# One decoder layer with product-key experts: table rows on one DMA queue, and the samples' retention in two halves of a buffer

## The chip, the cores and the metric

The kernel runs on one core of one Trainium2 chip, as one launch. The metric is the device time of an execution in microseconds, lower is better. A core has TensorE (PE; its weight loads are shown as PEld), VectorE (DVE), ScalarE (ACT), GpSimd (POOL) and SyncE (SP). A DMA is asked for by an instruction in one engine's queue; in the profile `ACTq` and `SPq` are such instructions, and the transfers of each asking engine form a queue of their own (q1 for SyncE, q10 for ScalarE, q0 for GpSimd's gathers).

## What is computed

One layer of a hybrid decoder for 512 tokens of a prompt and for 32 tokens of samples (8 samples of 4 tokens), width 1024. The input projection gives queries, keys, values and gates of a retention of four heads (head size 128), and the input of a causal depthwise convolution of width 31. Both halves are joined by an output projection, a residual and a normalisation. Then each token takes 16 of 16,384 experts for each of 8 heads, found by product keys. Cut to the parts that the change is near:

```python
# retention, for each chunk (a sample is one chunk of 4 tokens)
r_new   = chunk_decay * r + kv                  # state 128 x 128 for each sample and head
o_cross = einsum('bnihd,bnhde,hi->bnihe', qc, r_prev, decay_in)
# experts
u   = take(peer_u, idx)                         # (tokens, heads, 16, 1024)
act = gelu(einsum('phkd,pd->phk', u, x))
vv  = take(peer_v, idx)
out = einsum('phk,phkd->pd', gate * act, vv)
```

The outputs are the layer's result for prompt and samples, the new retention states and the new convolution caches.

## The kernel before

**The front, up to about 480 us.** The projection runs in blocks of tokens, the samples beside one of the prompt's. `retain_s` (L384 to L424) is the retention of the samples. After a first product over all 32 tokens (L396) it walks over four pairs of samples. For each pair it takes one buffer of the pool tag `keys` (L400, `keys_or_scratch`, one buffer); ScalarE writes the pair's values, scaled so that only the sample's own tokens are left, into the second half of it (L403); ScalarE's queue loads the pair's states, 1 MB, into the first half (L404). Eight matmuls take the states into the output `po` (L408), four more form the products of keys and values, one for each head, 256 columns wide for two samples (L412; the trace shows each matmul of 32-bit data as two instructions, so x16 and x8 there), VectorE adds them to the decayed states (L413), and SyncE's queue stores the result (L415). As the tag has one buffer, a pair's first write waits for the store of the pair before. The instructions of these pairs stand between those of the convolution (L263 makes diagonal matrices on ScalarE, L264 are its matmuls, L269 its sums on VectorE). `small(...)` gives tiles of a pool with two buffers for each name; the name `on` is used by the head norm (L331) and in `caches`, too.

**The experts.** The tokens are split. For two blocks of 128 prompt tokens and for the samples the rows that each token chose are gathered: `gather` asks for one row of u and v for each token (L573, an indirect DMA on GpSimd, 1 MB for 128 tokens), VectorE forms the dot product (L576), ScalarE the activation and the weight (L580, L581), VectorE adds the weighted row (L586). `finish` (L589) normalises the sum `yt` and stores it on SyncE's queue (L596). For the other 256 tokens the table is read whole. It has 128 rows of u (`ut`) and 128 of v (`uv`), a row being 512 KB for 128 experts. `scores_of` (L781) loads a row of u and takes eight matmuls of 256 columns over it (L787, x16 in the trace); `v_row` (L917) loads a row of v and `v_products` (L922, L925) take four matmuls of 512 columns (x8), with the gate matrices `Ga` to `Gd`, which are built in between (L865 to L904). The rows are held in four buffers of the tag `uv`, so a load can start when PE has finished the row four earlier.

**What sets the order.** A scheduler orders the instructions of each engine in the front; in the back two generators run in turn, `phases` (rows) and `fetched` (gathers and `finish`), two steps of the second for one of the first. The queue that loads a row is chosen in turn:

```python
turns = cycle((nc.sync, nc.scalar))       # L774
next(turns).dma_start(u, a["ut"][e])      # L784
next(turns).dma_start(vt, a["uv"][e * NK:(e + 1) * NK, D:])   # L919
```

By this, SyncE and ScalarE ask for 128 rows each. The end is the last rows of v, the normalisation of the 256 tokens, and four stores (L986).

Of the kernel before, what the change touches and what calls it, by code (L numbers as in the profile page):

```python
# [2 lines left out]

# [12 lines left out]
AF = mybir.ActivationFunctionType  # L16
# [4 lines left out]
D = 1024  # L21
# [3 lines left out]
H, DH, C = 4, 128, 128  # L25
CW, CK = 512, 31
PH, NK, TK = 8, 128, 16
# [67 lines left out]
def tile_step(ctx: ExitStack, tc: tile.TileContext, a, o):  # L95
    nc = tc.nc
    V, S, T, G = nc.vector, nc.scalar, nc.tensor, nc.gpsimd
# [17 lines left out]
    def mmps():  # L115
        turn[0] += 1
        return banks[turn[0] % len(banks)].tile([128, 512], F32, name="mm")
# [7 lines left out]
    def cc(n):  # L125
        part, c, w = COFF[n]
        return cst[part][:, c:c + w]
# [21 lines left out]
    blk = fe.tile([128, 8 * (NR - NS) + 8 * NR], F32, name="blk")  # L149
# [16 lines left out]
    def behind(ins, other):  # L166
        tc.add_manual_dep(ins.ins, other.ins.name, mybir.DependencyInfo(
            mybir.DependencyClass.NoSync, mybir.DependencyReason.DATA), reason="order")

    def small(name, shape, dt=F32, bufs=2):  # L170
        return wk.tile(shape, dt, name=name, bufs=bufs)
# [146 lines left out]
    def head_norm(po, n, kind):  # L318

        st = small("hst", [128, H, 6])  # L320
        mv = small("hmv", [128, H, 2])
        for h in range(H):
            V.bn_stats(st[:n, h], po[:n, h * DH:(h + 1) * DH])
            V.bn_aggr(mv[:n, h], st[:n, h])
        rs = small("hrs", [128, H])
        V.tensor_mul(rs[:n], mv[:n, :, 1], cc("gq2_" + kind)[:n])
        rsqrt(rs[:n], rs[:n])
        V.tensor_mul(rs[:n], rs[:n], cc("gq_" + kind)[:n])
        nb = small("hnb", [128, H])
        V.scalar_tensor_tensor(nb[:n], mv[:n, :, 0], -1.0, rs[:n], op0=OP.mult, op1=OP.mult)  # L330
        on = small("on", [128, 512])  # L331
        for h in range(H):
            S.activation(on[:n, h * DH:(h + 1) * DH], po[:n, h * DH:(h + 1) * DH], AF.Identity,
                         bias=nb[:n, h:h + 1], scale=rs[:n, h:h + 1])
        return on

    def gate_heads(on, n, gT, c0):
        pt = mmps().rearrange("p (h t) -> p h t", h=H)
        for h in range(H):
            T.transpose(pt[:, h, :n], on[:n, h * DH:(h + 1) * DH], ident[:n, :n])  # L340
        V.tensor_mul(gT[:, :, c0:c0 + n], gT[:, :, c0:c0 + n], pt[:, :, :n])

    def k_tokens(kT, c0, n, kind):
        pt = mmps()
        kt = small("ktok", [128, 512], bufs=1)
        for h in range(H):
            T.transpose(pt[:n, h * DH:(h + 1) * DH], kT[:, h, c0:c0 + n], ident)
        for h in range(H):
            S.activation(kt[:n, h * DH:(h + 1) * DH], pt[:n, h * DH:(h + 1) * DH], AF.Copy,
                         scale=cc("kc_" + kind)[:n, h:h + 1])  # L350
        return kt
# [33 lines left out]
    def retain_s(qT, kT, v, gT, after):  # L385

        n = NS
        pa = mmps()
        for h in range(H):
            behind(T.matmul(pa[:n, h * n:(h + 1) * n], kT[:, h, 0:n], qT[:, h, 0:n], start=True, stop=True), after)  # L390
        sc = small("sc", [128, 512])
        V.tensor_mul(sc[:n, :H * n], pa[:n, :H * n], cc("mask_s")[:n])
        kt = k_tokens(kT, 0, n, "s")
        po = mmps()
        for h in range(H):
            T.matmul(po[:, h * n:(h + 1) * n], v[:n, h * DH:(h + 1) * DH], sc[:n, h * n:(h + 1) * n],  # L396
                     start=(h == 0), stop=False, skip_group_check=True)
        for b in range(0, SB, 2):
            room = keys_or_scratch()
            r0 = room[:, 0:D].rearrange("p (b h e) -> p b h e", b=2, h=H)  # L400
            vx = room[:n, D:].rearrange("p (b e) -> p b e", b=2)
            for j in range(2):
                S.activation(vx[:, j], v[:n], AF.Copy, scale=cc("blk")[:n, b + j:b + j + 1])  # L403
            nc.scalar.dma_start(r0, a["state_retention"][0, b:b + 2].rearrange("b h d e -> d b h e"))  # L404
            for h in range(H):
                for j in range(2):
                    cs = h * n + (b + j) * SQ
                    T.matmul(po[:, cs:cs + SQ], r0[:, j, h], qT[:, h, (b + j) * SQ:(b + j + 1) * SQ],  # L408
                             start=False, stop=(h == H - 1 and b + j == SB - 1), skip_group_check=True)
            for h in range(H):  # L410
                pk = mmps()[:, 0:256]
                T.matmul(pk, kt[:n, h * DH:(h + 1) * DH], vx[:, :, h * DH:(h + 1) * DH], start=True, stop=True)  # L412
                V.scalar_tensor_tensor(r0[:, :, h], r0[:, :, h], float(GAMMA[h] ** SQ),  # L413
                                       pk.rearrange("p (b e) -> p b e", b=2), op0=OP.mult, op1=OP.add)
            nc.sync.dma_start(o[4][0, b:b + 2].rearrange("b h d e -> d b h e"), r0)  # L415
        oT = small("oT", [128, 128], bufs=1)
        S.activation(oT[:, :H * n], po[:, :H * n], AF.Copy)
        pt = mmps()
        for h in range(H):
            T.transpose(pt[:n, h * DH:(h + 1) * DH], oT[:, h * n:(h + 1) * n], ident)  # L420
        on = head_norm(pt, n, "s")
        gate_heads(on, n, gT, 0)
# [68 lines left out]
    def keys_or_scratch():  # L491
        return sel[0].tile([128, 2 * D], F32, name="keys", bufs=1)
# [132 lines left out]
    n = NR  # L625
# [25 lines left out]
    on = head_norm(po, C, "p")  # L651
# [24 lines left out]
    for h0 in range(0, PH, 2):  # L676
        w = load_w(a["w_query"], h0 * 256)
        qq = small("qe", [128, 4, 128], bufs=1)
        for hs in ([h0], [h0 + 1]) if h0 == 0 else ([h0, h0 + 1],):
# [7 lines left out]
            led = led or [c]  # L687
    conv_s(yS)
    retain_s(qS, kS, vs[0], gS, last0)

    banks[:] = [ps]
# [29 lines left out]
    xrs, pms, room = {}, {}, keys_or_scratch()  # L721
# [49 lines left out]
    ln2 = [bc_row("lng", a["ln2_g"], D), bc_row("lnb", a["ln2_b"], D)]  # L771
    GW = {2: gap.tile([128, EG[2], ND], F32, name="Ga")}

    turns = cycle((nc.sync, nc.scalar))  # L774

    def place(e):

        g = max(i for i in range(4) if E0S[i] <= e)
        return GW[g][:, e - E0S[g]]

    def scores_of(e):  # L781

        u = uvp.tile([128, D], F32, name="uv").rearrange("p (k e) -> p k e", k=8)
        next(turns).dma_start(u, a["ut"][e])  # L784
        sp = pdn.tile([128, ND], F32, name="sp")
        for k in range(8):
            T.matmul(sp, u[:, k], x1T[:, k, NG2:], start=(k == 0), stop=(k == 7))  # L787
        return sp
# [19 lines left out]
    for g in range(2):  # L808
# [9 lines left out]
        p = mmps().rearrange("p (q t) -> p q t", q=4)  # L818
# [13 lines left out]
    for e in range(E0S[2], E0S[3]):  # L832
        S.activation(place(e), scores_of(e), AF.Gelu)
# [3 lines left out]
    for e in range(EG[0]):  # L837
        S.activation(place(e), scores_of(e), AF.Gelu)
# [43 lines left out]
    def s_stage(e, n=ND):  # L882

        sp, G_ = scores_of(e), place(e)
        W = dw_.tile([128, ND], F32, name="W")
        S.activation(W[:, :n], sp[:, :n], AF.Gelu)
        if n < ND:
            S.activation(G_[:, n:], sp[:, n:], AF.Gelu)
        V.tensor_mul(G_[:, :n], G_[:, :n], W[:, :n])
# [26 lines left out]

    def v_row(e):  # L917
        vt = uvp.tile([128, D], F32, name="uv")
        next(turns).dma_start(vt, a["uv"][e * NK:(e + 1) * NK, D:])  # L919
        return vt  # L920

    def v_products(e, vt, b):  # L922
# [5 lines left out]
    def v_stage(e):  # L928
        vt = v_row(e)
        for b in range(2):  # L930
            v_products(e, vt, b)

    def phases():
        for e in range(EG[0]):
            v_stage(e)
            yield
        gbs.close()
        gd = ctx.enter_context(tc.tile_pool(name="gd", bufs=1, side="right", reuse_waits="tile"))
        GW[3] = gd.tile([128, EG[3], ND], F32, name="Gd")
        b = last_keys()  # L940
        more = iter(range(E0S[3], NK))
        for e in range(E0S[1], E0S[3]):
            v_stage(e)
            if next(b, "end") == "end":
                for _ in range(1):
                    k = next(more, None)
                    if k is not None:
                        s_stage(k)
            yield
        for e in range(E0S[3], NK - UV):  # L950
            v_stage(e)
            yield
        ends = [(e, v_row(e)) for e in range(NK - UV, NK)]
        for b in range(2):
            for e, vt in ends:
                v_products(e, vt, b)
                yield
# [75 lines left out]
```

## Time and profile before

| | |
|---|---|
| runs | 1601.7, 1597.08, 1602.1 us; median 1601.7 |
| profiled execution | 1610.35 us, of which the span is 1608.6 and 1.75 lie outside it |
| mean granted TensorE clock | 0.968 |
| loads of rows by queue | ut: 80 on ACTq, 48 on SPq; uv: 48 on ACTq, 80 on SPq |
| bytes moved | 503.75 MB, 313 GB/s on average over the span |

The profile is of one execution. A row of a table by stages gives the stretch in us, its length, the busy time of each engine with the number of instructions in brackets, the clock granted to TensorE as a share of the full one, the busy share of the DMA engines and what they moved. A row of the timeline gives the start, the duration, the engine, the line, the operation, what it writes and reads, the shapes, how many of a kind are drawn together (x4), and in square brackets the idle time of the engine before it with what ended it. A row of waits gives engine and line, what was waited for, and total, number and longest of the waits. A row of DMA queues gives packets, MB, and the share of the time of 16 DMA engines.

### The profile page before, as it was taken

What the parts mean: (1) busy time and instruction counts of PE and PEld (TensorE: products, weight loads), DVE (VectorE), ACT (ScalarE), POOL (GpSimd) and SP (SyncE); (2) the same over time, 40 slices, a digit from 0 to 9 for tenths busy, and PEclk for the clock granted to TensorE, in tenths of its full rate; (3) what the DMA queues carried; (4) which work ended last, traced back from release to release, by engine and by line L of the source; (5) the groups of instructions that cost most, each with busy time, mean ns of one, the idle gap of its engine ahead of it and who ended that gap; (6) DMA issues with size and microseconds to landing.
All of it is one profiled execution on the core that took longest, in us unless ns stands there. A gap on an engine that the chain in (4) does not pass through costs nothing.

```text
span 1608.6 us, 20726 instructions
## 1 busy us (share of the span) xinstructions
PE 1481.2 (92%) x7014; PEld 1016.0 (63%) x7014; DVE 1223.1 (76%) x3158; ACT 601.6 (37%) x1687; POOL 394.4 (25%) x335
## 2 busy tenths in 40 slices
PE   6899989996879997999999997989999999999997
PEld 6788557554666666888888885434566655644443
DVE  3939989989774999999866989667777677776642
ACT  2225352244221323333623799512994111111100
POOL 1001323433431222221122100233223223333200
PEclk9999989997989999999999997999999999999999
DMA  9458678997789768998699721989999999999972
GB/s 356 178 200 350 247 252 294 345 356 253 262 338 360 254 232 311 351 333 313 221 390 375 282 80 58 374 344 417 375 350 387 418 406 420 416 423 424 425 263 94
DMA packets 99542, 503.75 MB, mean 313 GB/s; under 512 B 10183, under 2 KB 21191, under 8 KB 56549
## 3 DMA queue, kind: packets, MB, share of 16 engines
q0 software_dynamic: 42240, 305.12, 48.9%
q1 hardware_dynamic: 32317, 122.84, 20.5%
q10 hardware_dynamic: 24880, 74.47, 12.4%
q8 instruction: 55, 0.90, 0.2%
q14 instruction: 50, 0.41, 0.1%
HBM read 497.03 MB, written 5.80 MB: 313 GB/s over the span
## 4 chain that ended last, share of the span: by engine, by line
PE 32%; DMA 28%; DVE 20%; issue 12%; POOL 5%; ACT 2%; ACTq 0%; POOLq 0%; SPq 0%; DVEq 0%
DMA g<-in_uv_dram,Ib 15%; PE pB L925 12%; PE sp L787 9%; DMA g<-in_uv_dram,I 8%; DVE acc L586 5%; PE mm L199 5%; POOL g L573 4%; DVE g L576 3%; PE mm L878 2%; DMA uv<-in_uv_dram 2%; DMA g<-in_w_in_dram 2%; DVE score L506 1%; PE mm L309 1%; PE mm L476 1%; DVE iu L505 1%
## 5 line engine op out<-in xcount | busy, mean ns | idle before, releaser
L787 PE MATMUL sp<-x1T,uv 128*128 128x256 f32 x2048 | 465.9, 383 | 25.4 <-DMA uv<-in_ut_dram 13.1
L787 PEld LDWEIGHTS sp<-x1T,uv 128*128 128x128 f32 x2048 | 386.0, 191 | 99.1 <-issue 27.7
L586 DVE SCALAR_TENSOR_TENSOR acc<-g,wgt,acc 128x1024 f32<-128x1024 f32 x285 | 364.8, 1280 | 102.1 <-ACT wgt L581 101.3
L573 POOL DMA_INDIRECT g<-in_uv_dram,I x128 | 177.1, 1384 | 451.9 <-DVE acc L586 253.5
L580 ACT ACTIVATE act<-act 128x1 f32<-128x1 f32 x288 | 57.8, 201 | 611.5 <-DVE g L576 599.9
L573 POOL DMA_INDIRECT g<-in_uv_dram,Ib x128 | 158.2, 1236 | 431.7 <-DVE acc L586 238.0
L576 DVE SCALAR_TENSOR_TENSOR g<-g,x1g 128x1024 f32<-128x1024 f32 x160 | 195.6, 1224 | 89.1 <-DMA g<-in_uv_dram,Ib 60.5
L576 DVE SCALAR_TENSOR_TENSOR g<-g,x 128x1024 f32<-128x1024 f32 x128 | 155.4, 1215 | 38.2 <-DMA g<-in_uv_dram,I 38.0
L199 PE MATMUL mm<-x1T,w 128*128 128x384 f32 (+1 forms) x512 | 177.6, 503 | 0.0
L925 PE MATMUL pB<-uv,Ga 128*128 128x512 f32 x352 | 157.2, 594 | 4.5 <-DMA uv<-in_uv_dram 4.4
L865 ACT ACTIVATE off<-row,e1T 128x128 bf16<-128x128 bf16 x512 | 157.7, 388 | 1.6 <-PE sp L787 0.6
L199 PEld LDWEIGHTS mm<-x1T,w 128*128 128x128 f32 x512 | 97.5, 192 | 71.9 <-issue 39.5
L925 PE MATMUL pB<-uv,Gb 128*128 128x512 f32 x256 | 117.4, 613 | 6.1 <-DMA uv<-in_uv_dram 5.6
L925 PEld LDWEIGHTS pB<-uv,Ga 128*128 128x128 f32 x352 | 66.3, 190 | 77.2 <-issue 67.4
L925 PE MATMUL pB<-uv,Gd 128*128 128x512 f32 x256 | 111.0, 593 | 2.9 <-DMA uv<-in_uv_dram 2.9
L925 PEld LDWEIGHTS pB<-uv,Gd 128*128 128x128 f32 x256 | 48.3, 190 | 65.4 <-issue 60.5
L925 PEld LDWEIGHTS pB<-uv,Gb 128*128 128x128 f32 x256 | 48.7, 196 | 64.2 <-issue 55.3
L878 PEld LDWEIGHTS <-A 128*128 128x128 bf16 x1536 | 64.4, 99 | 35.3 <-issue 26.3
L878 PE MATMUL mm<-B,A 128*128 128x96 bf16 (+1 forms) x1536 | 67.8, 196 | 11.6 <-DVE Gc L904 10.0
L873 DVE TENSOR_TENSOR B<-M,gtT 128x768 bf16<-128x768 bf16 (+1 forms) x192 | 69.5, 418 | 11.6 <-PE mm L878 11.6
L925 PE MATMUL pB<-uv,Gc 128*128 128x512 f32 x160 | 73.0, 601 | 0.0
L867 ACT ACTIVATE A<-off 128x1024 bf16<-128x1024 bf16 x64 | 67.4, 1053 | 14.4 <-PE mm L878 10.3
(279 smaller groups left out, 1701.5 us busy)
## 6 DMA issues: line engine op xcount, KB each, us to landing
uv<-in_ut_dram ACTq DMA_DIRECT2D x80, 512.0 KB
uv<-in_uv_dram SPq DMA_DIRECT2D x80, 512.0 KB
uv<-in_ut_dram SPq DMA_DIRECT2D x48, 512.0 KB
uv<-in_uv_dram ACTq DMA_DIRECT2D x48, 512.0 KB
w<-in_w_in_dram SPq DMA_DIRECT2D x18, 1024.0 KB
w<-in_w_query_dram SPq DMA_DIRECT2D x16, 1024.0 KB
w<-in_w_out_dram SPq DMA_DIRECT2D x7, 1024.0 KB
g<-in_uv_dram,I POOLq DMA_INDIRECT x128, 8.0
```

Source lines behind the costliest of these rows:

```text
L199: T.matmul(p[:, :n], w[m // 2][:, k, (m % 2) * 128:(m % 2 + 1) * 128], xT[:, k, c0:c0 + n], start=(k == 0), stop=(k == 7))
L309: mm = T.matmul(p[:n, q * 256:(q + 1) * 256], xT[:, k, c0:c0 + n], w[q][:, k, :], start=(k == 0), stop=(k == 7))
L573: G.indirect_dma_start(out=t, out_offset=None, in_=a["uv"], in_offset=bass.IndirectOffsetOnAxis(ap=idx[:, k:k + 1], axis=0))
L576: dot = V.scalar_tensor_tensor(t[:, :D], t[:, :D], 1.0, x1, op0=OP.mult, op1=OP.mult, accum_out=act[:, 0:1])
L580: S.activation(act[:, 1:2], act[:, 0:1], AF.Gelu)
L586: V.scalar_tensor_tensor(acc, v, wgt, acc, op0=OP.mult, op1=OP.add)
L787: T.matmul(sp, u[:, k], x1T[:, k, NG2:], start=(k == 0), stop=(k == 7))
L865: S.activation(off[:, t], row, AF.Abs, bias=e1T[:, t1 + t:t1 + t + 1])
L867: S.activation(A, off, AF.Relu, bias=1.0, scale=-1.0)
L873: V.tensor_tensor(B[:, q], M, pairs_of(gtT[:, q], t1).to_broadcast([128, TB // 2, ne, 2]), op=OP.mult)
L878: T.matmul(pt[:, t % nt], A[:, t - t1], B[:, q, (t - t1) // 2, :, t % 2], start=(q == 0), stop=(q == 2))
L925: T.matmul(pB[b][q], W[:, b * 128:(b + 1) * 128], vt[:, q * 512:(q + 1) * 512], start=False, stop=(e == NK - 1), skip_group_check=True)
```

## The change

Rows: `turns` is dropped, and `nc.sync` asks for all 256. Retention: one buffer of `keys` is taken for all four pairs; pair 0 and pair 2 put their states into its first half, pairs 1 and 3 into its second; the scaled values of each sample go to a tile `on` of their own, and so the 256-column matmul at L412 becomes two of 128 columns.

```diff
+        room = keys_or_scratch()
         for b in range(0, SB, 2):
-            room = keys_or_scratch()
-            r0 = room[:, 0:D].rearrange("p (b h e) -> p b h e", b=2, h=H)
-            vx = room[:n, D:].rearrange("p (b e) -> p b e", b=2)
+            r0 = room[:, b // 2 % 2 * D:(b // 2 % 2 + 1) * D].rearrange("p (b h e) -> p b h e", b=2, h=H)
+            vx = [small("on", [128, 512]) for _ in range(2)]
             for j in range(2):
-                S.activation(vx[:, j], v[:n], AF.Copy, scale=cc("blk")[:n, b + j:b + j + 1])
+                S.activation(vx[j][:n], v[:n], AF.Copy, scale=cc("blk")[:n, b + j:b + j + 1])
...
                 pk = mmps()[:, 0:256]
-                T.matmul(pk, kt[:n, h * DH:(h + 1) * DH], vx[:, :, h * DH:(h + 1) * DH], start=True, stop=True)
+                for j in range(2):
+                    T.matmul(pk[:, j * DH:(j + 1) * DH], kt[:n, h * DH:(h + 1) * DH], vx[j][:n, h * DH:(h + 1) * DH],
+                             start=True, stop=True)
...
-    turns = cycle((nc.sync, nc.scalar))
...
-        next(turns).dma_start(u, a["ut"][e])
+        nc.sync.dma_start(u, a["ut"][e])
...
-        next(turns).dma_start(vt, a["uv"][e * NK:(e + 1) * NK, D:])
+        nc.sync.dma_start(vt, a["uv"][e * NK:(e + 1) * NK, D:])
```

In the order of instructions that follows, the loads of the states of pairs 0 and 1 stand together on ScalarE's queue, those of pairs 2 and 3 wait for the stores of pairs 0 and 1, the scaling (L403) waits for the matmuls of the pair before (L412), and on SyncE's queue the three stores of `yt` have 52, 116 and 245 row loads ahead of them (55, 116 and 246 before, counting both queues).

More of the change, by code (lines that the diff above doesn't have):

```diff
@@ L1 @@
 from contextlib import ExitStack
-from itertools import cycle
 import numpy as np
```

## The prediction

> **What bounds the kernel now.** I read the page's busy times first, then a table of the span cut into stages, then the waits, the timeline and the DMA of the stages that the diff touches.
>
> ```profile
> span 1608.6 us, 20726 instructions
> PE 1481.2 (92%) x7014; PEld 1016.0 (63%) x7014; DVE 1223.1 (76%) x3158; ACT 601.6 (37%) x1687; POOL 394.4 (25%) x335
> ```
> ```profile
> core 0: us, PE busy (x) PEld busy (x) DVE busy (x) ACT busy (x) POOL busy (x), PEclk, DMA share, GB/s
> 150.00:200.00 50.00, 48.04 (x178) 29.17 (x177) 47.01 (x150) 22.10 (x41) 16.27 (x9) 1.00 0.75 277
> 200.00:230.00 30.00, 22.99 (x70) 14.55 (x71) 23.89 (x54) 14.90 (x45) 7.11 (x6) 0.77 0.77 253
> 350.00:480.00 130.00, 99.42 (x489) 77.38 (x488) 105.73 (x184) 46.24 (x116) 51.45 (x43) 0.87 0.78 289
> 480.00:800.00 320.00, 305.07 (x1326) 235.53 (x1325) 285.42 (x1098) 108.45 (x274) 68.43 (x56) 0.99 0.81 298
> 1200.00:1420.00 220.00, 209.71 (x852) 136.82 (x851) 157.10 (x217) 54.33 (x192) 68.25 (x58) 1.00 1.00 408
> 1420.00:1530.00 110.00, 103.50 (x244) 45.32 (x243) 75.46 (x92) 15.20 (x61) 33.95 (x30) 1.00 1.02 424
> ```
> PE's 92% is an average over different limits. Up to 200 us PE and VectorE are both nearly full (48.04 and 47.01 of 50). From 200 to 230 neither is (22.99 and 23.89 of 30), and the granted clock falls to 0.77: that hole is the samples' retention. From 350 to 480 neither is full, from 480 to 800 PE is. From 1200 to 1530 the DMA is (share 1.00 and 1.02) with PE at 95% and 94%: two limits side by side. So a microsecond saved in the front can be lost between 350 and 480, and one saved in the back must get past the DMA.
>
> **Retention: two places.** Each of the four pairs of samples now takes the one buffer of its pool: scaled values (L403) in its second half, loaded states (L404) in its first. The next pair begins only when the store of the updated states (L415) has landed. The timeline of pair 1:
>
> ```profile
> 187.56 5.32 PE L199 MATMUL mm<-x1T,w 128*128 128x384 f32 x16
> 188.50 0.73 DVE L413 SCALAR_TENSOR_TENSOR keys<-keys,mm 128x256 f32<-128x256 f32 x2
> 189.26 0.40 SPq L415 DMA_DIRECT2D out_dram<-keys  x1
> 190.01 0.58 ACT L231 ACTIVATE sg<-mm,cols 128x384 f32<-128x384 f32 x1
> 192.72 5.33 PE L264 MATMUL mm<-u_p,dg 128*128 128x384 f32 x16
> 200.69 0.72 ACT L403 ACTIVATE keys<-v,cst 32x512 f32<-32x512 f32 x1 [9.92 <-DVE blk L269]
> 200.75 0.38 ACTq L404 DMA_DIRECT2D keys<-in_state_retention_dram  x1
> 202.08 1.91 PE L412 MATMUL mm<-keys,ktok 32*128 32x256 f32 x4 [4.04 <-ACT keys L403]
> 208.92 3.58 PE L408 MATMUL mm<-samples,keys 128*128 128x4 f32 x16 [4.93 <-DMA keys<-in_state_retention_dram]
> 212.36 7.17 PE L264 MATMUL mm<-u_p,dg 128*128 128x384 f32 x16
> 219.46 1.13 PE L412 MATMUL mm<-keys,ktok 32*128 32x256 f32 x4
> 239.74 1.84 PE L408 MATMUL mm<-samples,keys 128*128 128x4 f32 x16
> ```
> The store is issued at 189.26, right after its last L413, and ScalarE starts the next L403 at 200.69, 11.4 us later. The row names VectorE as releaser, but L269 had been done for long; what came late is the store. PE has emptied its queue at 198.05 (192.72 + 5.33), loses 4.04 us before L412 and 4.93 before L408, the load taking 8.2 us (200.75 to 208.92). Until it is warm it also runs slowly: L412 1.91 us against 1.13, L264 7.17 against 5.33, L408 3.58 against 1.84, together 4.4 us.
>
> Does the change remove that? Pair 1 no longer waits for the store: its states are asked for together with those of pair 0. But the order of instructions moves too. Pair 1's first L412 stand ahead of the sixteen L199 that are at 187.56 in the trace, and wait for its L403, which on ScalarE stand just behind L231, done at 190.6 (190.01 + 0.58), and take 2 x 0.72: 192.0. PE waits there from 187.6 to 192.0, 4.4 us. Then L412 (1.1), the L199 (5.3) and fourteen L264 (14 x 5.33/16 = 4.7) lead to 203.1, and there the order already has the first L408 of pair 2. Its states wait for the store of pair 0, whose L413 keep their place in VectorE's order: they are asked for at about 200.7 and land at 208.9 as before. PE waits 5.8 us. The sum is 10.2 us of waiting against 8.97: the wait has gone from pair 1 to pair 2. In exchange pair 1's L408 are done by then (1.84 us), less two L264 (0.7): PE is 1.1 us further on.
>
> Pair 3 waits in the same way for the store of pair 1. Its last L413 come behind those L408, at about 213; with 11.4 and 8.2 us as above its states land at about 233, and PE, with some 22 us of work in between at those durations, asks at about 232. ScalarE's queue stands at that load until 225, and behind it are eight of the L263 tiles for L264; I reckon some 2 us of PE's there. Behind the earlier wait for the store, of 9 us or so, stand activations and weights of two gathers, which stood behind L403 before.
>
> Two small costs. The first two L403 go ahead of other work of ScalarE at about 111 us: 2 x 0.72 = 1.4 us, counted in full. And L412 becomes two matmuls of 128 columns, 64 rather than 32:
>
> ```profile
> 112.99 1.06 PE L375 MATMUL mm<-g,ktok 128*128 128x128 f32 x8
> ```
> That is 0.13 us each, 64 x 0.13 = 8.5 us against 32 x 1.13/4 = 9.0: nothing. So the front: 1.1 gained, 2 and 1.4 lost, -2.3 us. Between the bounds: all waits and slow matmuls gone, 8.97 + 4.4 - 1.4 = 12 gained; or the wait for pair 3 as long as that of pair 2 with its slow clock, 5.8 + 4.4 = 10 lost on top. I take a loss of 1, since 350 to 480 has slack for the rest.
>
> On the clock, the Trainium skill (TensorE: Matmul & The Clock Gate, Part 1) says that idle windows of PE of some 3.4 us halve it until PE has been busy again for a window. The 0.77 of this stage agrees. By that rule the slow clock goes only if the single wait gets shorter than that, and by the estimate above it does not.
>
> **Table rows: one queue.** The 256 rows of 512 KB are asked for now by SyncE and ScalarE in turn, after by SyncE alone, into four buffers. The back:
>
> ```profile
> 1072.91 0.20 ACT L580 ACTIVATE act<-act 128x1 f32<-128x1 f32 x1 [4.13 <-DVE g L576]
> 1073.22 0.33 ACTq L919 DMA_DIRECT2D uv<-in_uv_dram  x1
> 1081.33 10.89 PE L925 MATMUL pB<-uv,Gb 128*128 128x512 f32 x19 [3.96 <-DMA uv<-in_uv_dram]
> 1310.86 3.60 PE L925 MATMUL pB<-uv,Ga 128*128 128x512 f32 x8
> 1312.89 0.33 ACTq L784 DMA_DIRECT2D uv<-in_ut_dram  x1
> ```
> ```profile
> PE sp L787 <- DMA uv<-in_ut_dram: 10.3, 9, 2.3
> ```
> ```profile
> PE pB L925 <- DMA uv<-in_uv_dram: 6.4, 6, 2.4
> ```
> The waits are those of 1200 to 1420 and of 1420 to 1530. A load on ScalarE's queue stands behind the activation of a gather: the one at 1073.22 comes right after an activation that had waited 4.13 us, and PE then waits 3.96 at 1081.33. In steady state the buffer is free at 1310.86, when PE turns to the next row, and the request comes at 1312.89, 2.0 us later. SyncE has nothing of the kind in its queue. Bounds: at the least nothing, since the DMA is full; at the most the DMA's slack, 408 GB/s in the one stage against 424 in the next, 220 x (1 - 408/424) = 8.3 us, with the 3.96: 12.3. I take 3, because the last gathers set where the end begins:
>
> ```profile
> 1549.56 6.37 ACTq L919 DMA_DIRECT2D uv<-in_uv_dram  x2
> 1552.01 1.22 DVE L456 TENSOR_TENSOR yt<-yt,lnb 128x1024 f32<-128x1024 f32 x1
> 1553.26 0.34 SPq L596 DMA_DIRECT2D out_dram<-yt  x1
> ```
> The store of the last gathered block (L596) is on SyncE, and eleven rows stand behind it in the changed kernel. From here to the end are 1608.6 - 1553.3 = 55.3 us, so PE's gains alone do not shorten the end; the gathers must finish earlier. Before, ScalarE asked for a row at 1549.56, past that wait; after, it waits to 1553.6, 4 us, with three buffers (3 x 3.60 us) to cover it.
>
> **Against the change: the share of one ring.**
>
> ```profile
> q0 software_dynamic: 1925, 14.00, 66.3%
> q10 hardware_dynamic: 1007, 3.67, 17.9%
> q1 hardware_dynamic: 983, 3.58, 17.5%
> ```
> This is 1450 to 1500. q0 are the gathers, 14.00 MB in 1925 packets (7.3 KB each), q1 SyncE and q10 ScalarE (3.6 KB): q0 has about as many packets as both row queues together. A row takes PE 3.60 us, so it needs 146 GB/s. If the rings took turns packet by packet, one row ring beside the gathers would get 424 x 3.6/(3.6 + 7.3) = 140 GB/s, 3.74 us for a row. I count no loss in the sum, because the gathers gain what the rows lose and end earlier.
>
> The Trainium skill (DMA: Bandwidth & Descriptors, Queues, rings and completion order) says that each DMA engine does go round the queues packet by packet. No run here shows it yet for one row ring beside gathers.
>
> **The sum.** 1 us lost in the front, 3 gained by the rows. The profiled execution (1610.35 us, 1608.6 of it span) lies 8.65 above the median of the runs, 1601.7, so I expect a like one at about 1608, and a median of 1601.7 - 2 = 1599.7, say **1600**.
>
> **The rivals.** For these, the DMA issues of 800 to 900 (first fence) and of 1200 to 1420:
>
> ```profile
> uv<-in_ut_dram ACTq DMA_DIRECT2D x14, 512.0 KB
> uv<-in_ut_dram SPq DMA_DIRECT2D x14, 512.0 KB
> ```
> ```profile
> uv<-in_uv_dram SPq DMA_DIRECT2D x30, 512.0 KB
> uv<-in_ut_dram ACTq DMA_DIRECT2D x28, 512.0 KB
> ```
> B, faster: the rows' waits go and the gathers end earlier with a fuller DMA, 12.3 us, while the front costs nothing: 1589. For it: the waits for rows (16.7 us in two stages) and every second request 2 us late; against it: the DMA's shares of 1.00 and more.
>
> C, slower, by the ring's share. It decides where rows come at PE's pace beside gathers: one ring gives a row in 3.74 us, PE wants one in 3.60, 0.14 on each. That is 30 rows in 1420 to 1530 (110/3.6) and 28 in 800 to 900 (3.57 each), 58 x 0.14 = 8.1 us; with the front's 2.3 it is 10.4, and 1612. For it: the packet counts; against it: from 1200 to 1420 the 58 rows come at 220/58 = 3.79 us each anyway, slower than one ring would give them.
>
> D, the two places do not do what they say or do it fully: the wait only moves to pair 2, which is in the sum; or pair 1's early states free PE of both waits, 12 us, when the store lands much sooner than the 11.4 us before. Then 1587, which is counted with B.
>
> **How the numbers follow.** What a measurement of this kernel tells from no change is 0.3%, 4.8 us. Forecast 0.36, its own range 1595 to 1607, of which 0.04 is faster and 0.02 slower by more than that; B with D 0.32; C 0.32. Faster: 0.04 + 0.32 = 0.36. Same: 0.30. Slower: 0.02 + 0.32 = 0.34. The range takes in the times of B and D and of C, and the 2 us by which C grows if more rows than those counted are short: 1586 to 1614.
>
> **What would show it.** Right: around 187 to 192 us a wait of L412 for L403 of some 4 us, at about 203 one of L408 for its states of some 6, the clock below 1.00 from 200 to 230; no row load on ScalarE's queue and rows asked for within 0.5 us after PE leaves a buffer; no 4 us wait near 1081. Wrong: neither wait in the front (D); the last yt at 1545 or earlier and the end 10 us earlier (B); waits of L925 and L787 for rows that grow over 16.7 us in the two stages, with q0's share over 66% (C).

## The result and the profile after

| | before | after |
|---|---|---|
| median of 16 runs each | 1600.92 us (1596.51 to 1605.35) | 1609.87 us (1603.54 to 1613.48) |
| ratio, 95% interval | | 1.0059 [1.0046, 1.0073] |
| profiled execution | 1610.35 us in the prediction; a second one 1598.17 us (span 1596.4) | 1609.28 us (span 1607.5); a second one 1610.61 us (span 1608.8) |

The change costs 9 us, where the prediction had expected a gain of some 2; the time lies inside its range. The profile of before that the prediction read was of an execution slower than all 16 runs. So the comparisons below are against a second profile of before. The two profiles of before lie up to 6 us apart in the front and 12 at the end, and a single pair of profiles is not trusted with less than that.

The profile page of after, its first rows and the issues that differ. A row of the last two gives what is written and read, the queue, the number and the size:

```profile
span 1607.5 us, 20855 instructions
PE 1501.6 (93%) x7046; PEld 1018.6 (63%) x7046; DVE 1223.6 (76%) x3158; ACT 604.8 (38%) x1687; POOL 374.7 (23%) x335
...
uv<-in_ut_dram SPq DMA_DIRECT2D x128, 512.0 KB
uv<-in_uv_dram SPq DMA_DIRECT2D x128, 512.0 KB
...
keys<-in_state_retention_dram ACTq DMA_DIRECT2D x4, 512.0 KB
```

All rows are SyncE's now. The last row also corrects a figure of the text above: a pair's states are 512 KB, not 1 MB; nothing in the sum rested on it. The stages of after (busy time of each engine, clock, DMA share, GB/s):

```profile
150.00:200.00 50.00, 50.00 (x209) 32.34 (x208) 48.82 (x161) 20.66 (x39) 13.18 (x8) 0.97 0.77 284
200.00:230.00 30.00, 26.99 (x90) 17.04 (x89) 27.66 (x60) 18.32 (x45) 7.37 (x7) 0.83 0.88 299
350.00:480.00 130.00, 98.80 (x474) 75.75 (x473) 107.77 (x186) 45.81 (x114) 54.06 (x44) 0.87 0.80 290
1200.00:1420.00 220.00, 217.96 (x881) 135.87 (x880) 161.11 (x228) 60.96 (x205) 61.05 (x59) 1.00 1.01 417
1420.00:1530.00 110.00, 108.64 (x241) 43.08 (x240) 74.51 (x90) 15.22 (x61) 27.77 (x30) 1.00 1.02 424
```

From 150 to 230 us PE is busier than in the first profile of before (77.0 of 80 against 71.0), PE is nearly without holes from 1200 to 1530 us (217.96 of 220 and 108.64 of 110), and the kernel is slower all the same.

**The front.** The timeline of after around pairs 1 to 3 (in this and the other timelines only the rows that matter are shown; the import at the top is gone, so L402 is now the scaling, L403 the load, L407 the matmuls over the states, L416 the store):

```profile
183.02 1.32 ACT L402 ACTIVATE on<-v,cst 32x512 f32<-32x512 f32 x2
189.16 0.40 SPq L416 DMA_DIRECT2D out_dram<-keys  x1
192.25 1.15 PE L412 MATMUL mm<-on,ktok 32*128 32x128 f32 x8
200.10 0.37 ACTq L403 DMA_DIRECT2D keys<-in_state_retention_dram  x1
206.29 0.70 PE L407 MATMUL mm<-samples,keys 128*128 128x4 f32 x4 [3.01 <-DMA keys<-in_state_retention_dram]
206.92 2.07 PE L412 MATMUL mm<-on,ktok 32*128 32x128 f32 x8
231.14 1.84 PE L407 MATMUL mm<-samples,keys 128*128 128x4 f32 x16
```

Pair 1 waits for nothing. Pair 2's load is asked for when pair 0's store has landed (189.16 to 200.10, 10.9 us) and PE waits 3.01 us for it. Pair 3 waits for nothing.

In the second profile of before the waits that the change was to remove are small. These are pair 1 and pair 3 there:

```profile
199.88 3.17 PE L408 MATMUL mm<-samples,keys 128*128 128x4 f32 x16 [0.80 <-DMA keys<-in_state_retention_dram]
265.38 3.57 PE L408 MATMUL mm<-samples,keys 128*128 128x4 f32 x16 [2.96 <-DMA keys<-in_state_retention_dram]
```

Pair 1 costs 0.80 us of waiting there and 8.97 in the first profile, and yet the two profiles stand 0.2 us apart at 291 us. So a wait in this stage is not worth its length in time.

**The out-projection's normalisations.** The longest of PE's waits from 350 to 480 us, in after (columns: total, times, longest), then in the second profile of before:

```profile
PE mm L488 <- DVE xr L457: 13.8, 1, 13.8
PE mm L488 <- DVE lmv L450: 7.0, 1, 7.0
PE mm L339 <- ACT on L332: 6.5, 2, 5.0
```
```profile
PE mm L340 <- ACT on L333: 13.3, 2, 11.8
PE mm L487 <- DVE xr L456: 10.3, 1, 10.3
PE mm L487 <- DVE lrs L452: 4.8, 1, 4.8
```

The rows of L488 (before L487) are the transposes that wait for VectorE to finish the normalisation of a block. The one released by `xr` is the last block, the other the samples' block (its releaser named by an earlier step of it). Together 20.8 us against 15.1. The wait of the head norm (L339, before L340) went the other way, from 13.3 to 6.5, so the sum of the waits in this stage does not give the time lost in it; the starts of the same instruction, compared further down, do. Timeline of after at the last normalisation:

```profile
465.06 1.04 PE L488 MATMUL mm<-cst,keys 128*128 128x128 f32 x8
471.32 1.23 DVE L577 SCALAR_TENSOR_TENSOR g<-g,x 128x1024 f32<-128x1024 f32 x1 [5.13 <-DMA g<-in_uv_dram,I]
472.47 0.69 DVE L449 BATCH_NORM_STATS2 lst<-mm 128x6 f32<-128x512 f32 x1
...
474.35 0.69 DVE L449 BATCH_NORM_STATS2 lst<-mm 128x6 f32<-128x512 f32 x1
...
479.86 1.09 PE L488 MATMUL mm<-cst,xr 128*128 128x128 f32 x4 [13.76 <-DVE xr L457]
```

and of the second profile of before:

```profile
457.57 1.04 PE L487 MATMUL mm<-cst,keys 128*128 128x128 f32 x8
457.71 0.70 DVE L448 BATCH_NORM_STATS2 lst<-mm 128x6 f32<-128x512 f32 x1
...
465.69 1.23 DVE L576 SCALAR_TENSOR_TENSOR g<-g,x 128x1024 f32<-128x1024 f32 x1 [3.70 <-DMA g<-in_uv_dram,I]
...
468.88 1.09 PE L487 MATMUL mm<-cst,xr 128*128 128x128 f32 x4 [10.28 <-DVE xr L456]
```

PE runs its previous transposes (keys) and then has nothing. In after VectorE's next instruction is a gather's dot product (L577) that waits 5.13 us for its rows from DMA, and the first statistics (L449), which ran at 465.67 in a variant below, stand behind it. In the second profile of before they came at once (457.71); a dot stood further inside the normalisation and waited 3.70 us. The diff touches neither line: the order of each engine's front is written down anew by the scheduler whenever something in it changes.

**The rows.** Waits of PE for rows, 1200 to 1420 and 1420 to 1530 of after:

```profile
PE sp L786 <- DMA uv<-in_ut_dram: 0.3, 1, 0.3
```
```profile
PE pB L924 <- DMA uv<-in_uv_dram: 0.8, 2, 0.5
```

10.3 and 6.4 us have gone (in the second profile of before 7.6 and 4.5), and no row waits in ScalarE's queue. The DMA queues in 1420 to 1530 (packets, MB, share), after and then the second profile of before:

```profile
q0 software_dynamic: 4265, 31.03, 66.9%
q1 hardware_dynamic: 4266, 15.53, 34.5%
```
```profile
q0 software_dynamic: 4218, 30.63, 66.1%
q10 hardware_dynamic: 2157, 7.84, 17.7%
q1 hardware_dynamic: 2165, 7.88, 17.6%
```

One ring takes as many packets as the gathers (one more), and 15.53 MB / 110 us = 141 GB/s. Two rings together had 143.

### The profile page after: what moved, and what is told of

The parts are those of the page before. It is cut to its first block, busy times and chain, and to the rows that moved or that the text cites. A ratio compares the mean times of both kernels' runs of the same rounds, so it can differ in the third digit from the quotient of the medians.

```text
span 1607.5 us, 20855 instructions
## 1 busy us (share of the span) xinstructions
PE 1501.6 (93%) x7046; PEld 1018.6 (63%) x7046; DVE 1223.6 (76%) x3158; ACT 604.8 (38%) x1687; POOL 374.7 (23%) x335
## 5 line engine op out<-in xcount | busy, mean ns | idle before, releaser
L574 POOL DMA_INDIRECT g<-in_uv_dram,I x128 | 171.0, 1336 | 446.0 <-DVE acc L587 230.0
L577 DVE SCALAR_TENSOR_TENSOR g<-g,x1g 128x1024 f32<-128x1024 f32 x160 | 195.3, 1223 | 87.1 <-DMA g<-in_uv_dram,Ib 57.4
L574 POOL DMA_INDIRECT g<-in_uv_dram,Ib x128 | 140.9, 1101 | 453.5 <-DVE acc L587 318.5
L577 DVE SCALAR_TENSOR_TENSOR g<-g,x 128x1024 f32<-128x1024 f32 x128 | 155.2, 1213 | 31.0 <-DMA g<-in_uv_dram,I 30.9
L924 PE MATMUL pB<-uv,Ga 128*128 128x512 f32 x352 | 162.0, 603 | 0.1
L877 PE MATMUL mm<-B,A 128*128 128x96 bf16 (+1 forms) x1536 | 68.1, 196 | 17.0 <-DVE Gc L903 10.3
```

The costliest lines, as they stand in the source:

```text
L574: G.indirect_dma_start(out=t, out_offset=None, in_=a["uv"], in_offset=bass.IndirectOffsetOnAxis(ap=idx[:, k:k + 1], axis=0))
L577: dot = V.scalar_tensor_tensor(t[:, :D], t[:, :D], 1.0, x1, op0=OP.mult, op1=OP.mult, accum_out=act[:, 0:1])
L877: T.matmul(pt[:, t % nt], A[:, t - t1], B[:, q, (t - t1) // 2, :, t % 2], start=(q == 0), stop=(q == 2))
L924: T.matmul(pB[b][q], W[:, b * 128:(b + 1) * 128], vt[:, q * 512:(q + 1) * 512], start=False, stop=(e == NK - 1), skip_group_check=True)
```

## The experiments

Ratios are to before's runs on the same chip, with their 95% interval. `behind(x, y)` is an ordering hint: the scheduler places x after y on its engine, without a wait.

**1. One part at a time.** `rows_only` is before with

```diff
-        next(turns).dma_start(u, a["ut"][e])
+        nc.sync.dma_start(u, a["ut"][e])
-        next(turns).dma_start(vt, a["uv"][e * NK:(e + 1) * NK, D:])
+        nc.sync.dma_start(vt, a["uv"][e * NK:(e + 1) * NK, D:])
```

and `ret_only` is after with these lines put back, the retention alone. `before_again` and `after_again` are the two kernels unchanged, for second profiles.

> Only the queue of the table rows is changed (all on SyncE); the retention is that of the kernel before. Theory R (the loss of 0.59% comes from the rows: one ring beside the gathers gets a smaller share, and rows stand behind the stores of yt): ratio about 1.006, and waits of L925 and L787 for their rows of more than 17 us between 1200 and 1530. Theory F (the loss comes from the front, where the retention's work is in another order): ratio 0.998 to 1.001, and waits for rows under 10 us. My forecast's terms, 3 us gained by the rows and 1 lost in the front, would give 0.998.

> Only the retention is changed (two halves of one buffer, a tile of scaled values for each sample); rows alternate between SyncE and ScalarE as before. Theory F: ratio about 1.006. Theory R: 0.998 to 1.001. In both, PE's wait for the states of pair 2 is about 3 us, as in the changed kernel's profile, against 9 us of waits for pair 1 before.

> The kernel before once more, for a second profile of it: the first one's execution took 1610.35 us, above all sixteen runs without a profile (1596.5 to 1605.4). Both theories: the places where this profile differs from the first show how much two executions of one kernel differ by themselves; I expect up to 10 us in the front and the ends within 8 us.

> The changed kernel once more, for a second profile. Theory R: between 1200 and 1530 its rows are later than in both profiles of the kernel before. Theory F: it is late already when the first row is multiplied (about 500 us), by 4 to 9 us, as the first profile was by 4.5.

Measured: rows_only 0.9998 [0.9977, 1.0019], ret_only 1.0085 [1.0055, 1.0116]. The rows are worth nothing either way, and the loss is the retention's. Waits of PE's weight loads in 1420 to 1530, before_again and then after, show where a part of the waits that went is found again:

```profile
PEld pB L925 <- DMA uv<-in_uv_dram: 7.7, 7, 1.6
```
```profile
PEld pB L924 <- DMA uv<-in_uv_dram: 12.8, 16, 0.9
```

Fewer long waits became more short ones: 7 of up to 1.6 us, 7.7 in all, against 16 of up to 0.9, 12.8 in all. The DMA share was 1.01 and 1.02 in this stage, so it had no room to bring the rows faster.

**2. Which part of the retention, and is it the order?** `after_stats` is after with the 74th dot behind the last statistics, `before_late_stats` is before with the reverse, `vals_only` has the values' tiles but the states in one place as before (with alternating rows, as ret_only), and `ret_planned` (alternating, too) has both parts of the retention, with each pair's scaling and load placed behind the store of the pair before:

```diff
 # after_stats, in gather; lasts = the last two L449
+            if x1 is x1_0 and k == 73:
+                behind(dot, lasts[1])
 # before_late_stats, in gather
+            if x1 is x1_0 and k == 73:
+                for s in lasts:
+                    behind(s, dot)
 # vals_only, against ret_only
-        room = keys_or_scratch()
         for b in range(0, SB, 2):
+            room = keys_or_scratch()
-            r0 = room[:, b // 2 % 2 * D:(b // 2 % 2 + 1) * D].rearrange(...)
+            r0 = room[:, 0:D].rearrange(...)
 # ret_planned, against ret_only
+                if b:
+                    behind(act, store)
+            if b:
+                behind(load, store)
```

> The changed kernel with one order fixed: VectorE's dot product for the 74th gather of the first block stands behind the last statistics of the front's normalisation, as in the kernel before. Theory O (the loss comes from the order in which the front is written down anew, in two places: about 5 us at 300 to 310 and about 3.5 us at 457 to 470, where the statistics stand behind a dot that waits for its gather): 3 to 5 us faster than the changed kernel, ratio about 1.003 to 1.004. Theory Q (the loss comes from the retention itself: ScalarE's queue standing at loads that wait for stores, and states that come late): ratio still about 1.006 to 1.008.

> The kernel before with the opposite order in this one place: the last statistics stand behind the dot product of the 74th gather, nothing else is changed by hand. Theory O: 3 to 4 us slower, ratio about 1.002, if the front's end is carried to the end of the kernel; theory Q: 1.000.

> Rows alternate as before; of the retention only the tiles for scaled values are changed (L403, L412), the states keep one place, so that each pair's load still waits for the store before. Theory O: the order is written down anew here too, but with 73 dots ahead of the last statistics as before, so most of the loss should be absent: ratio 0.998 to 1.004. Theory Q: the states come as late as before and nothing else changes, ratio about 1.000; a ratio of 1.008 would say that the scaled values' tiles alone bring the loss.

> Rows alternate as before; the retention has both parts of the change, but the scheduler is told to place each pair's scaling and load behind the store of the pair before, as the order was. On the chip nothing waits for that store until pair 2. Theory O: pair 1's waits of PE (9 us and the slow clock) are gone or under 3 us, the later order stays near that of the kernel before, and the ratio is 0.994 to 1.002. Theory Q: ScalarE's queue stands at the loads of pairs 2 and 3 as in the changed kernel, ratio 1.004 or more.

Measured: after_stats 1.0094 [1.0072, 1.0117], a miss (1.003 to 1.004 was expected); before_late_stats 1.0053 [1.0033, 1.0073], more than the 1.002 expected; vals_only 1.0071 [1.0042, 1.01], a miss (0.998 to 1.004); ret_planned 1.0012 [0.999, 1.0033]. With the same tiles, matmuls and loads but another order ret_planned is level with before, so the work of the new retention does not cost the time by itself. vals_only, whose states come as late as before, is as slow as ret_only, so the two places are not needed for the loss. And one dot put ahead of the statistics, the only edit, costs before 0.53%; in its profile the last matmul of the output projection is still 1.4 us ahead of before_again, and the first row's 8.1 behind. Why the reverse did not help after shows in the timeline of after_stats:

```profile
465.67 1.29 DVE L451 BATCH_NORM_STATS2 lst<-mm 128x6 f32<-128x512 f32 x2
471.16 1.23 DVE L579 SCALAR_TENSOR_TENSOR g<-g,x 128x1024 f32<-128x1024 f32 x1 [4.20 <-DMA g<-in_uv_dram,I]
472.31 0.20 DVE L452 BATCH_NORM_AGGREGATE lmv<-lst 128x2 f32<-128x12 f32 x1
476.15 1.23 DVE L579 SCALAR_TENSOR_TENSOR g<-g,x 128x1024 f32<-128x1024 f32 x1 [3.64 <-DMA g<-in_uv_dram,I]
478.50 0.15 DVE L455 SCALAR_TENSOR_TENSOR lrs<-lmv,lrs 128x1 f32<-128x1 f32 x1
...
481.94 1.09 PE L490 MATMUL mm<-cst,xr 128*128 128x128 f32 x4 [16.23 <-DVE xr L459]
```

The statistics are early now, but the next two steps stand behind dots that wait 4.20 and 3.64 us: PE waits 16.23 us instead of 13.8. Freeing the first link of the chain only moved the wait to the next.

**3. The last normalisation freed.** In layer_norm the last addition is kept, and the dots from the 74th on go behind it; the same on before. `planned_chain` is the whole change with ret_planned's order and the dots from the 73rd on behind it.

```diff
-            V.tensor_add(t[:n, c], t[:n, c], b[:n, c])
+            hold.append(V.tensor_add(t[:n, c], t[:n, c], b[:n, c]))
...
+            if x1 is x1_0 and k >= 73:
+                behind(dot, lasts[1])
```

> The changed kernel with one order fixed more fully than in the run before: all of VectorE's dot products from the 74th gather of the first block on stand behind the last addition of the front's last normalisation, not only behind its statistics. Theory N (what the changed kernel loses against the kernel before is lost where the last normalisation's six steps on VectorE stand behind dots that wait for their gathers, about 7 us in the changed kernel's second profile against none before the statistics in the kernel before): PE's wait for that normalisation falls from 14 us to 7 or less and the time from 1.006 to about 1.000 to 1.002. Theory M (the loss is spread over the whole front and its order; one place is worth nothing, since VectorE as the bound gives it back later): ratio 1.004 or more.

> The kernel before with the same order fixed: dots from the 74th on behind the last normalisation. There one dot stood inside the chain and waited 3.7 us for its gather. Theory N: 3 to 4 us faster than the kernel before, ratio 0.997 to 0.998. Theory M: 1.000.

> Both parts of the change (all rows on SyncE, two places and a tile for each sample), with two orders fixed: scaling and loads of each pair placed behind the store of the pair before, and dots from the 73rd on behind the last normalisation. With the first alone the front was 12 us ahead of the kernel before at the last matmul of the output projection and lost 8 of them at the last normalisation, behind a dot that waited 6.4 us. Theory N: those 8 us stay, ratio 0.992 to 0.997. Theory M: 0.999 to 1.003.

Measured: after_chain 1.0018 [0.9995, 1.0041], before_chain 0.996 [0.9935, 0.9985], planned_chain 0.9938 [0.9913, 0.9963]. Both gain some 0.4%, and a difference of 0.6% stays. The gain of before_chain is not that of the wait it was built to shorten: in its new order a dot that waits for its gather stands ahead of the statistics, and PE waits as long for the last block as in before_again (10.28):

```profile
457.63 1.23 DVE L578 SCALAR_TENSOR_TENSOR g<-g,x 128x1024 f32<-128x1024 f32 x1 [3.41 <-DMA g<-in_uv_dram,I]
458.78 0.70 DVE L450 BATCH_NORM_STATS2 lst<-mm 128x6 f32<-128x512 f32 x1
...
466.02 1.08 PE L489 MATMUL mm<-cst,xr 128*128 128x128 f32 x4 [10.90 <-DVE xr L458]
```

In after_chain the wait for the last block did fall, from 13.8 us to 6.3; that for the samples' block is still 7.9.

**4. The samples' normalisation too, and the rows once more.** `after_chain2` adds to after_chain the line below; `planned_alt` is planned_chain with the rows alternating.

```diff
+            elif x1 is x1_0 and k >= 63:
+                behind(dot, firsts)
```

> As the run with the last normalisation ahead, and in addition the dots from the 64th on stand behind the normalisation of the 32 sample rows (about 415 to 435 us), inside which three dots stood in the changed kernel and PE waited 7.9 us, against 3.2 with the order of the kernel before. Theory N2 (the rest of the difference, 0.58% between the two kernels with the last normalisation ahead, is lost in this place): ratio 0.996 to 0.999. Theory M2 (it is lost elsewhere, in the stage at 300 to 330 or behind 500): 1.001 to 1.003 as without.

> The fastest version so far (0.9938), but with the rows asked for by SyncE and ScalarE in turn, as before. If the rows on one queue are worth nothing, as alone (0.9998), 0.992 to 0.996; if their gain comes out only with a faster front, 0.996 to 0.998.

Measured: after_chain2 1.0059 [1.0036, 1.0082], a miss of both theories (0.996 to 0.999, 1.001 to 1.003), planned_alt 0.9936 [0.9915, 0.9957]. The first is inconclusive: the new order put two dots back into the last normalisation, so the samples' block waits no more, and the last one waits 13.5 us. Its profile is of the slowest of its 12 executions (1623.28 us).

The second repeats, in a faster kernel, that the rows' queue makes no difference (0.9938 and 0.9936).

**5. Both freed.** With `k >= 70` in place of 73, on after and on before:

> The run before put the sample rows' normalisation ahead, but the new order then had two dots again inside the last normalisation (PE waited 13.5 us there), so it could not tell. Here both are free of dots: dots from the 64th on behind the first, from the 71st on behind the last. Theory N2: ratio 0.996 to 0.999, as the kernel before with the same done to it (0.9960). Theory M2, that the rest is lost in the stage at 300 to 330 and behind 500: 1.001 to 1.003, as with the last normalisation alone (1.0018).

> The kernel before with both normalisations free of dots (the same two orders as in the run before on the changed kernel, which gave 0.9942). If the change itself is worth nothing either way once the dots are out of the way: 0.992 to 0.996. If the new order of the front also loses the 5 us at 300 to 330 for good: 0.988 to 0.991. If the two places and the single queue gain by themselves: 0.997 or more.

Measured: after_chain3 0.9942 [0.9916, 0.9967], before_chain3 0.9965 [0.9945, 0.9986]. In the medians the difference between the two kernels is gone (1594.97 and 1594.98 us); after_chain3 is faster than either theory expected, and the intervals overlap. Waits for the last block in after_chain3 and in before_chain3, neither of which waits for the samples' block:

```profile
PE mm L490 <- DVE xr L459: 4.3, 1, 4.3
```
```profile
PE mm L489 <- DVE xr L458: 4.3, 1, 4.3
```

PE's waits for the normalisations of the samples' and the last block, added up in each profile (the last wait may begin before 480 and end behind it), and the start of the first row's matmul against before_again, beside the time of each kernel. after_again is after once more:

| kernel | PE's waits there, us | first row, us | ratio |
|---|---|---|---|
| before_again / rows_only | 15.1 / 14.7 | 0 / +1.8 | 1 / 0.9998 |
| after / after_again / ret_only | 20.8 / 21.4 / 21.3 | +10.3 / +14.3 / +9.7 | 1.0059 / 1.0059 / 1.0085 |
| vals_only / before_late_stats / after_stats | 17.0 / 22.3 / 22.4 | +9.5 / +8.1 / +13.1 | 1.0071 / 1.0053 / 1.0094 |
| after_chain / before_chain | 14.2 / 14.1 | -0.7 / -3.4 | 1.0018 / 0.996 |
| after_chain3 / before_chain3 | 4.3 / 4.3 | -3.0 / -15.3 | 0.9942 / 0.9965 |
| ret_planned | 18.0 | -4.1 | 1.0012 |
| after_chain2 | 13.5 | +11.1 | 1.0059 |
| planned_chain / planned_alt | 7.1 / 8.4 | -17.0 / -8.9 | 0.9938 / 0.9936 |

The waits go with the time only roughly. after_chain and before_chain wait alike and lie 0.6% apart; before_chain3 waits 9.8 us less than before_chain and is no faster; ret_planned waits 18.0 us and is level with before, having gained 7.2 us by 291 us. The start of the rows does better: the kernels that begin them 8 us late or later have ratios of 1.0053 and more, those within 2 us or ahead 1.0018 and less (the prediction's profile of before, +5.7, lies between them). So the loss is there when the rows begin. A lead at this point is not carried to the end in full: before_chain3 begins the rows 12.3 us ahead of after_chain3 and has the same median. Its profile is of the fastest of its 12 executions, 7.8 us under the median, which may be a part of it; the rest is open.

Three versions beat both kernels: planned_alt (1592.33 us), planned_chain (1590.35) and after_chain3 (1594.97), with intervals that overlap. Two of the three have the change's rows, and one does not.

## Why the prediction was wrong, point by point

Where time is lost against before_again, by the start of the same instruction in each profile (us, from single executions; before_again's own start in the second column; the first profile of before is the prediction's; the 16 rope matmuls are those of the last block, from 291 us on):

```
                                before_again  before  rows_only  after  after_again  ret_only  after_chain3  before_chain3
first rope matmul                     291.0    +0.2     +0.3     -1.3     +1.3        -0.2       +2.9          -0.9
16th rope matmul                      328.0    +3.9     +0.3     +5.4     +9.0        +5.5       +8.3          -0.9
last out-projection matmul            457.4    +5.9     +2.3     +7.5    +10.0        +6.5       +3.7          -8.9
first row's matmul                    495.3    +5.7     +1.8    +10.3    +14.3        +9.7       -3.0         -15.3
first v row's matmul                  948.9    +8.6     +1.7     +9.2    +12.5        +9.4       -6.1         -10.6
```

**The retention, up to 230 us: right in kind, sizes too large.** The wait moved from pair 1 to pair 2, as forecast: the load was asked for at 200.10 (forecast 200.7) and PE waited 3.01 us (forecast 5.8; 4.6 in the second profile). The wait of L412 for the scaled values, forecast at 187 to 192 us with 4.4 us, did not come: ScalarE reached them at 183.02, not at 190.6, and L412 ran at 192.25 without one. Pair 3 had no wait. The upper bound of 12 us counted pair 1's 8.97 and the slow matmuls in full; before_again, with 0.80 us for pair 1, is only 0.2 us ahead at 291. At 291 us the three profiles with the new retention stand at -1.3, +1.3 and -0.2, in line with a sum near nothing there.

On the clock, the four L412 after the 3.01 us of waiting took 2.07 us against 1.15 at 192.25, and the stage was granted 0.83. The Trainium skill (TensorE: Matmul & The Clock Gate, Part 1) puts the idle window that halves the clock at some 3.4 us; the idle time of the weight loads was 3.63 us before that instruction and PE's own 3.01, so this trace does not tell which of the two counts. That the slow clock would stay in this stage, as the prediction had it, is borne out.

**The step that failed: "So the front: 1.1 gained, 2 and 1.4 lost", and "I take a loss of 1, since 350 to 480 has slack for the rest".** The sum priced the retention's instructions, its waits and the queues they passed, and put the order that the scheduler gives to all else in the front at nothing, without a reason. The front's term was -1 us; the kernel lost 9 (1609.87 - 1600.92, with the rows at nothing), and the rows began 10.3, 14.3 and 9.7 us late in the three profiles with the new retention. By the table these are lost in two places that the diff doesn't touch.

The first is the rope of the last block, from 291 to 328 us, with 5.7 to 7.7 us. PE's row in after with ScalarE's rows ahead of it, and then ScalarE's in before_again, in which PE waits for nothing here:

```profile
303.66 0.20 ACT L581 ACTIVATE act<-act 128x1 f32<-128x1 f32 x1 [2.34 <-DVE g L577]
...
304.09 0.56 ACT L218 ACTIVATE blk<-mm,cols 128x384 f32<-128x384 f32 x1
304.71 0.91 PE L208 MATMUL mm<-blk,cst 128*128 128x384 f32 x2 [2.43 <-ACT blk L218]
```
```profile
302.80 0.58 ACT L219 ACTIVATE blk<-mm,cols 128x384 f32<-128x384 f32 x1 [3.02 <-PE mm L199]
303.28 0.19 ACT L580 ACTIVATE act<-act 128x1 f32<-128x1 f32 x1
```

In after the rope's activation (L218) stands behind activations of gathers that wait for their dots; in before_again such an activation stands behind the rope's. Of the six profiles with before's order of the retention only the prediction's own loses time here (+3.7).

The second is the stage from 350 to 480, with the samples' and the last normalisation: from 328 us to the first row another 4.2 to 5.3 us are lost. The stage has idle time on PE, but that is waiting for chains on other engines, and these have no slack of their own. A dot that waits for its gather, with 5.13 us, stood ahead of the last normalisation, and the samples' wait went from 4.8 to 7.0.

That an order of this kind costs time is shown by before_late_stats, where one dot in the second place costs 0.53%; that the retention's work is not the cause, by ret_planned. How the 9 us divide between the two places is not shown. Holding the dots back behind both normalisations makes the kernels end alike, but after_chain3 still loses 5.4 us at the rope, and it begins the rows as far behind before_chain3 (12.3 us) as after behind before_again (10.3); the rope's place was not changed by itself. The new order, though not its waits, could be read before the run, had it been compared beyond the retention.

**The rows: +3 forecast, 0 measured** (0.9998 [0.9977, 1.0019]). The waits went as the prediction said, a row is asked for at once (1310.64 us, PE having left the buffer at 1310.55), and no 4 us wait near 1081 is left, but the DMA was full and gave the rows at the same rate. The last store of yt was not earlier either:

```profile
1550.23 0.34 SPq L597 DMA_DIRECT2D out_dram<-yt  x1
```

In the first profile of before it was at 1553.26, in the second at 1541.40. From it to the end it is 57.3 us, not 55.3: in all profiles with one queue this stretch is 57.3 to 59.0 us, in those with two 54.2 to 56.3. What causes the difference was not tried. The lower bound of that term, "at the least nothing, since the DMA is full", was the value to take.

**The rivals.** C's share of the ring came, and its loss did not. The Trainium skill (DMA: Bandwidth & Descriptors, Queues, rings and completion order) says that a DMA engine goes round its queues packet by packet, and 4265 packets against 4266 would fit that; 141 GB/s was measured where 140 was worked out. But two rings had no more, 143 GB/s, with 4322 packets beside 4218 of the gathers, so equal counts are no proof of turns. Three queues in turn would give two rings two packets in three; they took one in two, so something else than turns held them, most likely how soon buffers came free (not tried), and there was no share for one ring to lose. B fell with the rows. D's gain fell with the 3.01 us. The slower side that came true was none of those named: not a queue or a wait of the changed part, but the rest of the front in a new order.

## What to carry to other kernels

Where a scheduler writes the order of in-order engines, an edit costs what the whole new order costs. Compare the order of every engine up to the end of the scheduled stage, and look for instructions that wait on DMA or on its users (here the gathers' dots and their activations) standing ahead of or inside a short dependent chain that another engine waits for. Holding the dots back behind both normalisations was worth more (0.35% on before; on after 1.2%, from 1.0059 to 0.9942) than either part of the edit, though each such hint writes the whole order anew and one of them (after_chain2) gained nothing. Idle time of an engine is no slack where it waits for a chain on another; and compare two kernels by when the same instruction starts, since waits can move without the time moving. With the DMA full, shorter waits for the rows brought no time here.

## What the runs showed of the hardware that was not expected

One ring beside the gathers moves as much as two: 34.5% of the DMA's time and 141 GB/s against 35.3% (17.7 + 17.6) and 143. And one program's executions differ more than its medians do: before ran from 1596.51 to 1605.35 us in 16 runs and its profiled execution took 1610.35, with PE's waits for pair 1's states and values between 0.80 us (before_again) and 8.97 (the prediction's profile) in the profiles with before's order of the retention. A difference of 9 us had to be read from intervals, and from several profiles at the same instructions.
